# A transpose on one core: one TensorE wait per copying engine and step, a loop meant to fit one instruction fetch of 16 KB, and stores issued right behind their closing copy

## The chip, the cores and the metric

One core of one Trainium2 chip. The metric is device time in microseconds, median of several executions; the kernel before took 1264.57 us (three runs, 1264.06 to 1268.05). Profiles are single executions whose span, from first to last instruction, is about 2 us shorter than the time.

## The reference

```python
def setup_inputs():
    return {"x": np.random.randn(8192, 8192).astype(np.float32)}

def reference(x):
    return np.transpose(x)
```

268.4 MB have to be read and 268.4 MB written.

## The kernel before

The input goes through in 128 steps, each a tile of 128 rows by 4096 columns (2 MiB). TensorE transposes it in 32 blocks of 128 x 128 into four PSUM banks of eight; ScalarE copies banks 0 and 2, VectorE banks 1 and 3, into registers of SBUF ("windows"). Eight windows are open at a time and nine exist; each gathers eight steps, so that a store writes rows of 4 KB, and one closes per step. ScalarE issues all stores and, but for the first three, all loads.

```python
    NIN, NREG = 3, 9
    s_bank = [nc.alloc_semaphore(f"s_bank{q}") for q in range(NR // 2)]     # four banks
    # ...
        def transposes(k):
            nc.tensor.sem_inc(s_ld[k], -16).wait_op(s_ld[k], 16, "sem-ge")
            for h in range(NR // 2):
                nc.tensor.sem_inc(s_bank[h], -1).wait_op(s_bank[h], 1, "sem-ge")
                for b in range(2 * B):
                    # ... one transpose into bank h
                tr.then_inc(s_pe, 1)
    # ...
        with nc.Fori(0, T // NIN + 1, engines=pe, head_slot={pe[0]: 0}) as turn:
            with nc.tensor.If(turn > 0):
                transposes(NIN - 1)
            nc.tensor.wait_ge(s_id, 2)
            for k in range(NIN - 1):
                transposes(k)
    # ...
        for t, (s, c) in enumerate(chunks):
            closing = []
            for h in range(NR // 2):
                e = h % 2
                eng = (nc.scalar, nc.vector)[e]
                # ... open windows; wait for a free register (s_st)
                eng.wait_ge(s_pe, t * NR // 2 + h + 1)
                before = []
                if e == 0:
                    before, closing = closing, []
                # ... the copies of bank h; windows that end here go into `closing`
                for k in before:
                    store(*k)
            for k in closing:
                store(*k)
            if t + NIN < T:
                nc.scalar.wait_ge(s_pe, (t + 1) * NR // 2)
                load(t + NIN)
```

Of the kernel before, what the change touches and what calls it, by code (L numbers as in the profile page):

```python
# [24 lines left out]
def wide_dma(nc, eng, queue, out, in_):  # L25


    return eng.add_instruction(
        mybir.InstDMACopy(
            mode="Copy",  # L30
            name=nc.get_next_instruction_name(),
            engine=eng.engine,
            ins=[physical(in_)],
            outs=[physical(out)],
            queue=queue,
        )
    )


@with_exitstack  # L40
def kernel(
    ctx: ExitStack,
    tc: tile.TileContext,
    x: bass.AP,
    out: bass.AP,
):







    nc = tc.nc
    P = 128
    N, M = x.shape
    assert x.shape == out.shape[::-1]
    dt = x.dtype

    S = 32  # L60
    B = 4
    W = 8
    NR = S // B
    NIN = 3
    NREG = 9
    CH = N // P
    J = S * P

    with tc.tile_critical():  # L69
        nc.alloc_sbuf_tensor("pad", [P, 32], dt)  # L70
        ident = nc.alloc_sbuf_tensor("ident", [P, P], dt).ap()
        ins = [nc.alloc_sbuf_tensor(f"in{k}", [P, J], dt).ap() for k in range(NIN)]
        SIZE = B * W * P
        regs = nc.alloc_sbuf_tensor("regs", [P, NREG * SIZE], dt).ap()
        pss = [nc.alloc_psum_tensor(f"ps{k}", [P, 2 * B * P], dt).ap() for k in range(NR // 2)]

        s_id = nc.alloc_semaphore("s_id")
        s_ld = [nc.alloc_semaphore(f"s_ld{k}") for k in range(NIN)]
        s_st = [nc.alloc_semaphore(f"s_st{k}") for k in range(NREG)]
        s_bank = [nc.alloc_semaphore(f"s_bank{q}") for q in range(NR // 2)]  # L80
        s_pe = nc.alloc_semaphore("s_pe")
        s_cp = [nc.alloc_semaphore("s_cpa"), nc.alloc_semaphore("s_cpv")]

        nc.gpsimd.memset(ident, 0.0).then_inc(s_id, 1)  # L84
        nc.gpsimd.wait_ge(s_id, 1)
        nc.gpsimd.affine_select(  # L86
            out=ident,
            in_=ident,
            compare_op=mybir.AluOpType.not_equal,
            fill=1.0,  # L90
            base=0,
            pattern=[[-1, P]],
            channel_multiplier=1,
        ).then_inc(s_id, 1)

        chunks = [(s, c) for s in range(M // J) for c in range(CH)]

        def load(t):
            s, c = chunks[t]
            (nc.sync if t < NIN else nc.scalar).dma_start(  # L100
                out=ins[t % NIN], in_=x[c * P:(c + 1) * P, s * J:(s + 1) * J]
            ).then_inc(s_ld[t % NIN], 16)





        def transposes(k):
            nc.tensor.sem_inc(s_ld[k], -16).wait_op(s_ld[k], 16, "sem-ge")
            for h in range(NR // 2):  # L110
                nc.tensor.sem_inc(s_bank[h], -1).wait_op(s_bank[h], 1, "sem-ge")  # L111
                for b in range(2 * B):
                    j = (2 * h + b // B) * B * P + b % B
                    tr = nc.tensor.transpose(  # L114
                        pss[h][:, b * P:(b + 1) * P],
                        ins[k][:, j:j + B * P - B + 1:B],
                        ident,
                    )
                tr.then_inc(s_pe, 1)



        T = len(chunks)
        assert T % NIN == NIN - 1
        pe = [nc.tensor.engine]
        for h in range(NR // 2):
            nc.tensor.sem_inc(s_bank[h], 1)
        with nc.Fori(0, T // NIN + 1, engines=pe, head_slot={pe[0]: 0}) as turn:
            with nc.tensor.If(turn > 0):
                transposes(NIN - 1)  # L130
            nc.tensor.wait_ge(s_id, 2)
            for k in range(NIN - 1):
                transposes(k)

        for t in range(NIN):
            load(t)

        copied = [0, 0]
        free = list(range(NREG))
        stored = [0] * NREG  # L140
        window = {}

        def store(q, e, count):
            t0, r, parts = window.pop(q)
            nc.scalar.wait_ge(s_cp[e], count)
            base = 0
            for s, a, z in parts:
                rows = (z - a) * P
                j0 = s * J + q * B * P
                dst = out[j0:j0 + B * P, a * P:a * P + rows]  # L150
                dst = dst.rearrange("(q b) i -> q b i", q=P)
                src = regs[:, r * SIZE + base:r * SIZE + base + B * rows]
                base += B * rows
                if any(stored):
                    st = wide_dma(nc, nc.scalar, "qActDynamicHW", dst, src)
                else:
                    st = nc.scalar.dma_start(
                        out=dst, in_=src.rearrange("q (b i) -> q b i", b=B)
                    )
                st.then_inc(s_st[r], 16)  # L160
                stored[r] += 1
            free.append(r)

        def closes(w, t):
            t0, r, parts = w
            return t + 1 == t0 + sum(z - a for _, a, z in parts)

        for t, (s, c) in enumerate(chunks):
            closing = []
            for h in range(NR // 2):  # L170
                e = h % 2
                eng = (nc.scalar, nc.vector)[e]

                place = []
                for q in (2 * h, 2 * h + 1):
                    if q not in window:



                        span = (q - c) % W + 1  # L180
                        r = free.pop(0)
                        parts = [(s, c, min(c + span, CH))]
                        if c + span > CH and t + span < T:
                            parts.append((s + 1, 0, c + span - CH))
                        window[q] = (t, r, parts)
                        if stored[r]:
                            eng.wait_ge(s_st[r], 16 * stored[r])
                    t0, r, parts = window[q]
                    k = [p[0] for p in parts].index(s)
                    base = r * SIZE + B * P * sum(z - a for _, a, z in parts[:k])  # L190
                    _, a, z = parts[k]
                    place.append((base + (c - a) * P, (z - a) * P))
                ends = [q for q in (2 * h, 2 * h + 1) if closes(window[q], t)]
                gap = place[1][0] - place[0][0]
                runs = [(0, 1)]
                if place[0][1] != place[1][1] or abs(gap) >= 2 ** 15:
                    runs = [(0,), (1,)]
                eng.wait_ge(s_pe, t * NR // 2 + h + 1)  # L198
                before = []
                if e == 0:  # L200
                    before, closing = closing, []
                for u in runs:
                    off, dist = place[u[0]]
                    dims = [list(regs.ap[0]), [gap, len(u)], [dist, B], [1, P]]
                    o = bass.AP(regs.tensor, regs.offset + off, dims)
                    i = pss[h][:, u[0] * B * P:(u[-1] + 1) * B * P]
                    i = i.rearrange("p (l b i) -> p l b i", b=B, i=P)
                    cp = nc.scalar.copy(out=o, in_=i) if e == 0 else nc.vector.tensor_copy(out=o, in_=i)  # L208
                    mine = [q for q in ends if q - 2 * h in u]
                    if mine:  # L210
                        cp.then_inc(s_cp[e], 1)
                        copied[e] += 1
                        closing += [(q, e, copied[e]) for q in mine]
                    if u is runs[-1]:
                        if mine:
                            eng.wait_ge(s_cp[e], copied[e])
                            eng.sem_inc(s_bank[h], 1)
                        else:
                            cp.then_inc(s_bank[h], 1)
                for k in before:  # L220
                    store(*k)
            for k in closing:
                store(*k)
            if t + NIN < T:
                nc.scalar.wait_ge(s_pe, (t + 1) * NR // 2)
                load(t + NIN)
        for r in range(NREG):
            nc.sync.wait_ge(s_st[r], 16 * stored[r])
# [30 lines left out]
```

## Time and profile before

| | kernel before |
|---|---|
| time, median of the first three runs | 1264.57 us |
| span of the profiled run | 1263.0 us |
| TensorE / VectorE / ScalarE busy | 747.5 / 316.0 / 262.9 us |
| bytes read + written, mean rate | 536.9 MB, 425 GB/s |
| from step to step, mid-run | 9.76 us |

Read the page from the engine shares down: when no engine is busy over 60% and the DMA row is all nines, the next question is what the DMA engines lose and where. "DMA share" is the mean over the core's 16 DMA engines. The lines are shown inside the prediction.

### The profile page before, as it was taken

To read this page: it belongs to the slowest core of one execution; us is meant where nothing else is said; L and a number is where in the kernel's file an instruction comes from. 1 tells how busy PE (TensorE), PEld (TensorE's weight loads), DVE (VectorE), ACT (ScalarE), POOL (GpSimd) and SP (SyncE) were. 2 spreads that over 40 slices of the span, in tenths; PEclk is the share of its full clock that TensorE was granted. 3 is DMA by queue.
4 is the path that set the end of the run, shared out by engine and by line. 5 is a ranking of instruction groups with operands and counts; after the bars stand their busy time and mean duration, and the time that the engine had idled before them with its cause. 6 is when DMAs were issued, how large, how long until landed. Compare 5 with 4: busy or idle time off the path is not lost. (4 is left out here: it accounts for less than half of the span.)

```text
span 1263.0 us, 10220 instructions
## 1 busy us (share of the span) xinstructions
PE 747.5 (59%) x4096; PEld 727.0 (58%) x4096; DVE 316.0 (25%) x311; ACT 262.9 (21%) x321; POOL 0.7 (0%) x6
## 2 busy tenths in 40 slices
PE   5665565565556555665556655656556655656561
PEld 5665555565556555665555655656556655656561
DVE  2322222222222222223222222222222222222220
ACT  2312121122212211222212121122212121122120
POOL 0000000000000000000000000000000000000000
PEclk9867877777776867677776686776877777776865
DMA  9999999999999999999999999999999999999998
GB/s 367 430 426 426 426 428 430 429 431 430 429 428 430 430 430 428 430 429 429 430 421 420 428 429 427 427 426 428 427 431 429 431 429 429 429 430 429 430 429 364
DMA packets 39275, 536.98 MB, mean 425 GB/s; under 512 B 4321, under 2 KB 4833, under 8 KB 6241
## 3 DMA queue, kind: packets, MB, share of 16 engines
q10 hardware_dynamic: 38832, 530.60, 98.9%
q1 hardware_dynamic: 432, 6.29, 1.2%
q14 instruction: 10, 0.07, 0.0%
q8 instruction: 1, 0.02, 0.0%
HBM read 268.44 MB, written 268.44 MB: 425 GB/s over the span
## 5 line engine op out<-in xcount | busy, mean ns | idle before, releaser
L114 PE MATMUL ps<-ident,in 128*128 128x128 f32 x4096 | 747.5, 365 | 489.0 <-PEq L111 489.0
L114 PEld LDWEIGHTS ps<-ident,in 128*128 128x128 f32 x4096 | 727.0, 219 | 509.3 <-issue 509.3
L208 DVE COPY regs<-ps 128x1024 f32<-128x1024 f32 (+1 forms) x311 | 316.0, 1034 | 921.8 <-PE ps L114 707.6
L208 ACT COPY regs<-ps 128x1024 f32<-128x1024 f32 (+1 forms) x320 | 261.6, 843 | 972.4 <-PE ps L114 693.6
L208 ACT ACT_TABLE_LOAD x1 | 1.3, 1283 | 0.9 <-SPq L69 0.9
L86 POOL TENSOR_SCALAR_AFFINE_SELECT ident<-ident 128x128 f32<-128x128 f32 x1 | 0.3, 294 | 0.2 <-POOL ident L84 0.2
L84 POOL MEMSET ident<- 128x128 f32 x1 | 0.2, 205 | 0.5 <-SPq L69 0.5
L243 POOL MEMSET const-bfloat16-1.0<- 128x1 bf16 x1 | 0.1, 103 | 0.0
L243 POOL MEMSET const-uint8-127<- 128x1 uint8 x1 | 0.1, 103 | 0.0
L243 POOL MEMSET const-float32-0.0<- 128x1 f32 x1 | 0.1, 99 | 0.2 <-issue 0.2
L243 POOL MEMSET const-float32-1.0<- 128x1 f32 x1 | 0.1, 99 | 0.0
## 6 DMA issues: line engine op xcount, KB each, us to landing
in<-in_x_dram ACTq DMA_DIRECT2D x125, 2048.0 KB, 22.5
out_dram<-regs ACTq DMA_DIRECT2D x114, 2048.0 KB, 18.3
out_dram<-regs ACTq DMA_DIRECT2D x4, 1792.0 KB, 15.3
in<-in_x_dram SPq DMA_DIRECT2D x3, 2048.0 KB, 13.1
out_dram<-regs ACTq DMA_DIRECT2D x4, 1536.0 KB, 14.3
out_dram<-regs ACTq DMA_DIRECT2D x4, 1280.0 KB, 15.0
out_dram<-regs ACTq DMA_DIRECT2D x4, 1024.0 KB, 14.5
out_dram<-regs ACTq DMA_DIRECT2D x4, 768.0 KB, 15.1
```

Of the source, the lines that this page charges most:

```text
L84: nc.gpsimd.memset(ident, 0.0).then_inc(s_id, 1)
L86: nc.gpsimd.affine_select(out=ident, in_=ident, compare_op=mybir.AluOpType.not_equal, fill=1.0, base=0, pattern=[[-1, P]], channel_multipl ...
L114: tr = nc.tensor.transpose(pss[h][:, b * P:(b + 1) * P], ins[k][:, j:j + B * P - B + 1:B], ident,)
L208: cp = nc.scalar.copy(out=o, in_=i) if e == 0 else nc.vector.tensor_copy(out=o, in_=i)
L243: nc = _bacc.Bacc("TRN2", target_bir_lowering=False, num_devices=1)
```

## The change

TensorE is to wait twice per step instead of four times, its program is to fit the first block of instructions fetched (so the placing of the loop's head, `head_slot`, is dropped), and each store is to leave as soon as its data is complete. "Block" stands here and below for what one instruction fetch of TensorE's brings: the traces of both kernels have one fetch on queue q8, of 16 KB.

```diff
-        s_bank = [nc.alloc_semaphore(f"s_bank{q}") for q in range(NR // 2)]
+        s_bank = [nc.alloc_semaphore("s_banka"), nc.alloc_semaphore("s_bankv")]
 ...
             for h in range(NR // 2):
-                nc.tensor.sem_inc(s_bank[h], -1).wait_op(s_bank[h], 1, "sem-ge")
+                if h < 2:
+                    n = NR // 4
+                    nc.tensor.sem_inc(s_bank[h], -n).wait_op(s_bank[h], n, "sem-ge")
 ...
-        for h in range(NR // 2):
-            nc.tensor.sem_inc(s_bank[h], 1)
-        with nc.Fori(0, T // NIN + 1, engines=pe, head_slot={pe[0]: 0}) as turn:
+        for e in range(2):
+            nc.tensor.sem_inc(s_bank[e], NR // 4)
+        nc.tensor.wait_ge(s_id, 2)
+        with nc.Fori(0, T // NIN + 1, engines=pe) as turn:
             with nc.tensor.If(turn > 0):
                 transposes(NIN - 1)
-            nc.tensor.wait_ge(s_id, 2)
 ...
-                before = []
-                if e == 0:
-                    before, closing = closing, []
+                closing = []
 ...   (copies of bank h; s_bank[h] becomes s_bank[e])
-                for k in before:
+                for k in closing:
                     store(*k)
-            for k in closing:
-                store(*k)
```

More of the change, by code (lines that the diff above doesn't have):

```diff
@@ L168 @@
         for t, (s, c) in enumerate(chunks):
-            closing = []
             for h in range(NR // 2):
@@ L216 @@
                             eng.wait_ge(s_cp[e], copied[e])
-                            eng.sem_inc(s_bank[h], 1)
+                            eng.sem_inc(s_bank[e], 1)
                         else:
-                            cp.then_inc(s_bank[h], 1)
-                for k in before:
+                            cp.then_inc(s_bank[e], 1)
+                for k in closing:
                     store(*k)
-            for k in closing:
-                store(*k)
             if t + NIN < T:
```

## The prediction

> **What bounds the kernel now.** I read the page first: engine shares, then the forty slices, then the bytes of the DMA queues. It says at once that no compute engine is the bound and that the DMA engines are.
>
> ```profile
> span 1263.0 us, 10220 instructions
> PE 747.5 (59%) x4096; PEld 727.0 (58%) x4096; DVE 316.0 (25%) x311; ACT 262.9 (21%) x321; POOL 0.7 (0%) x6
> DMA  9999999999999999999999999999999999999998
> GB/s 367 430 426 426 426 428 430 429 431 430 429 428 430 430 430 428 430 429 429 430 421 420 428 429 427 427 426 428 427 431 429 431 429 429 429 430 429 430 429 364
> q14 instruction: 10, 0.07, 0.0%
> HBM read 268.44 MB, written 268.44 MB: 425 GB/s over the span
> ```
>
> The DMA row is 9 in every slice but the last, and the rate stands at 420 to 431 GB/s in 38 slices of 40. The kernel must move 268.44 MB in and 268.44 MB out; 536.9 MB at 430 GB/s are 1248.5 us. The span is 1263.0, so about 14.5 us are all that is not full-rate transfer. The slices say where they lie (a slice is 31.6 us): the first, at 367, loses (430-367)/430 of 31.6 = 4.6 us; the last, at 364, loses 4.8; the 38 between lose about 5 together, some 3.5 of it in small sags of 1 to 4 GB/s and 1.4 in the two slices at 421 and 420, where the input's column half changes and the stores are short.
>
> Next I read the list of waits, to see whether anything waits for TensorE that matters, and then the time line of four steps.
>
> ```profile
> DVE regs L208 <- PE ps L114: 707.6, 204, 13.6
> ACT regs L208 <- PE ps L114: 693.6, 176, 9.7
> PE ps L114 <- PEq L111: 489.0, 127, 9.9
> ACT regs L208 <- DMA out_dram<-regs: 276.8, 50, 9.4
> DVE regs L208 <- DMA out_dram<-regs: 212.7, 30, 7.9
> ```
>
> TensorE waits 489.0 us in 127 waits, once before each of the 128 steps but one, 3.85 us each. The wait is booked to its own sequencer, at the line that waits for the load; the time line shows the rhythm:
>
> ```profile
> 602.25 6.43 PE L114 MATMUL ps<-ident,in 128*128 128x128 f32 x32 [3.55 <-PEq L111]
> 612.01 6.64 PE L114 MATMUL ps<-ident,in 128*128 128x128 f32 x32 [3.34 <-PEq L111]
> 621.77 5.37 PE L114 MATMUL ps<-ident,in 128*128 128x128 f32 x32 [3.12 <-PEq L111]
> ```
>
> Steps start 9.76 us apart whether TensorE took 6.64 or 5.37 us. A step moves 2 MiB in and 2 MiB out, 4.194 MB; over 9.76 us that is 430 GB/s. The step is the time of its transfers. Inside a step the 32 transposes come in one unbroken row: the three bank waits after the first cost nothing that the view can separate.
>
> Last, the end of the run in narrow windows (columns: window, its length, busy us of PE, PEld, DVE, ACT, POOL, granted clock, DMA share, GB/s):
>
> ```profile
> 1232.00:1234.00 2.00, 2.00 (x11) 2.00 (x10) 0.54 (x1) 0.83 (x2) 0.00 (x0) 0.50 1.02 434
> 1234.00:1236.00 2.00, 2.00 (x12) 2.00 (x11) 0.75 (x2) 0.83 (x2) 0.00 (x0) 0.55 0.85 360
> 1236.00:1238.00 2.00, 0.42 (x4) 0.23 (x2) 1.29 (x2) 0.24 (x1) 0.00 (x0) 1.00 0.45 187
> 1238.00:1240.00 2.00, 0.00 (x0) 0.00 (x0) 0.00 (x0) 0.00 (x0) 0.00 (x0) 0.81 1.10 454
> 1260.00:1261.00 1.00, 0.00 (x0) 0.00 (x0) 0.00 (x0) 0.00 (x0) 0.00 (x0) 0.50 0.16 66
> 1261.00:1263.00 2.00, 0.00 (x0) 0.00 (x0) 0.00 (x0) 0.00 (x0) 0.00 (x0) 0.50 0.00 0
> ```
>
> Here is the one place after the start where the DMA engines run dry: 1234 to 1238, at shares of 0.85 and 0.45.
>
> [...]So the first aim of the change, a program within one block, would matter if TensorE's loop refetched each turn. This trace speaks against that: 10 packets on the instruction queue in the whole span, for all engines, against 42 jumps back of the loop (43 turns of three steps).
>
> **The change part by part.**
>
> TensorE's waits. A step has four waits for PSUM banks now, and two after: one before the first bank for both of ScalarE's copies of the step before, one before the second for both of VectorE's. Per loop turn that removes 3 x 2 = 6 semaphore instructions or waits of about 3 x (1 + 4 + 64) = 207 (a transpose is a weight load and a matmul), leaving 201. Time gained: none on the path, since whatever TensorE saves becomes a longer wait for the load. What the coarser wait could cost: the first transposes of a step now need ScalarE's second copy of the step before. In the time line, TensorE ends at 608.68; ScalarE's last copy of the step ends at 608.72 and VectorE's at 610.07; the next step starts at 612.01. ScalarE is done 3.3 us before it is needed. In the worst pattern shown there (a copy held by a store until 626.45) the last ScalarE copy ends at 628.71 for a start at 631.53, 2.8 us of room. Cost 0.
>
> The fetch block and the wait for the identity moved ahead of the loop. The identity is ready at 1.7 us, the first load only just before TensorE's first instruction at 9.9 us. Gain 0 at the start, 0 later by the packet count above.
>
> The stores. Before, a store closed by the first bank is issued behind ScalarE's second copy of the step, two banks later; one closed by the second bank likewise behind that copy. After, each is issued right behind its closing copy. In the middle of the run this brings 2 of 8 stores forward by about two banks, some 3.4 us, and 2 by less. The order on the queue stays the same (store, then the step's load), and the queue is never empty there, so an earlier issue only lengthens the stay in the queue. Gain 0. In the last step it is different: all eight open windows close together, and nothing is loaded any more. ScalarE's copies of the first bank end at about 1232.8, but the first of the eight stores is issued only at 1236.36, and the DMA engines dry out meanwhile. With the change two stores, of 7 and 6 chunks by 256 KB = 1.79 + 1.54 (in units of 1024 KB: 3.3 in all, 3.41 MB, 7.9 us of work at 430 GB/s), are issued from about 1232.9 on, while the queue still has work. The dry time goes: (1-0.85) x 2 + (1-0.45) x 2 = 0.3 + 1.1 = 1.4 us; from the rates, (430-360)/430 x 2 + (430-187)/430 x 2 = 0.3 + 1.1 = 1.4 again.
>
> Sum: 0 + 0 + 0 - 1.4 = -1.4 us, from 1264.6 to 1263.2.
>
> **The rivals.**
>
> One: ScalarE now stands still in front of a store closed by VectorE's first bank until that copy is done, before its own second copy. VectorE is itself held by a store up to 7.9 us (30 waits). Then ScalarE's second copy, and with it TensorE's next start and the next load, come later. Against it: the load was always issued behind that store, so it moves by one copy, 0.6 to 1.1 us, in at most 2 steps of 8; and loads take 22.5 us from issue to landing, more than two steps, so they wait in a queue that others fill. If it bit each time, 32 steps by 1 us would be +32 us, 1295 us, slower by 2.5%.
>
> Two: the loop did refetch, or the four waits did stall TensorE, and TensorE gets faster. Its 489 us of idle time take it all: 0 us. For a real gain DMA itself would have to be freed, and that the bytes forbid: even with no loss at all it would be 1248.5 plus about 5 us of first and last latency, under 1% below now.
>
> Three: earlier stores mix with loads differently and the sags between 420 and 428 GB/s get better or worse. They are 5 us in all, so this moves the time by 2 or 3 us either way and I cannot tell which.
>
> **Range and chances.** The centre is 1264.6 - 1.4 = 1263.2, which I put at 1263.1, as an earlier fill may mend a sag. The three runs before spread from 1264.06 to 1268.05; with rival three's 2 to 3 us I take 1260 to 1266.5. Faster by 2% would be 1239.3, below the floor of the bytes at 430 GB/s: 0.01. Slower by 2% needs rival one nearly in full: 0.02. Within 2%: 0.97.
>
> **What would show it right or wrong.** The GB/s row should stay near 430 in the middle, steps 9.76 us apart. Near the end no window with a DMA share of 0.45; the first of the last stores issued some 3.5 us sooner than TensorE's last transpose; the span 1 to 2 us shorter. TensorE's idle time should stay near 490 us, with the same few instruction packets. The prediction is wrong if the middle slices fall below 420 (rival one: longer waits of TensorE for copies, dry DMA windows in mid-run), or if the span falls by more than 5 us, for then some wait that I call hidden did set the pace.

That 430 GB/s is the most to be had is the estimate from the slices, of which none is above 431 in that trace. The "about 5 us of first and last latency" fit the narrow windows of the same trace: against 430 GB/s the first 4 us lose 2.6 (0, 66, 197 and 360 GB/s), and 1260 to 1263 loses 2.8 (66, then 0 twice).

## The result, and the profile after

The changed kernel takes 1264.29 us (median of six, 1263.53 to 1265.31), the kernel before 1264.66 us (six, 1264.06 to 1268.05). The ratio of the fast runs is 0.9994, 95% interval 0.9981 to 1.0007: the same. (Such a ratio is the mean time of one kernel's fast runs over that of the other's in the same rounds, so not quite the ratio of the medians.) The predicted 1263.1 us, 1260 to 1266.5, held the time. Whether the gain of 1.4 us that it was built on came, the times alone cannot tell: the interval runs from 2.4 us faster to 0.9 slower. The traces tell, below: it did not.

From the page of the changed kernel:

```profile
span 1262.9 us, 9961 instructions
PE 742.7 (59%) x4096; PEld 721.8 (57%) x4096; DVE 316.1 (25%) x311; ACT 263.0 (21%) x321; POOL 0.7 (0%) x6
GB/s 381 429 430 420 429 431 428 430 429 431 428 430 430 431 428 429 430 430 430 426 425 414 429 430 429 430 430 430 428 430 430 431 428 430 430 430 429 430 427 339
q14 instruction: 9, 0.07, 0.0%
```

The span is 0.1 us shorter. The middle is at 430 GB/s as before. One slice, where the input's column half changes, reads 414 (before: 420), which is below the 420 that the prediction named as a sign of rival one; but the 38 middle slices together lose 3.7 us against 430 GB/s here and 4.6 before, so this is no sign of a slower middle. The last slice is at 339, where it was 364: the end carries less, not more. From its list of waits (who waited for whom, us in total, times, longest):

```profile
PE ps L117 <- PEq L114: 493.1, 128, 8.5
ACT regs L208 <- DMA out_dram<-regs: 260.3, 45, 9.2
DVE regs L208 <- DMA out_dram<-regs: 214.8, 30, 7.9
ACT regs L208 <- DVE regs L208: 47.1, 13, 4.0
```

TensorE's idle time is 493 us where it was 489. ScalarE now waits 47.1 us for VectorE's copies, a row that the kernel before does not have; its waits for stores went down by 16.5. Rival one of the prediction is thus in the trace, and costs nothing that the times resolve.

The end of the changed kernel in the narrow windows that the prediction used, and then the one window of the kernel before that the prediction left out:

```profile
1232.00:1234.00 2.00, 2.00 (x11) 2.00 (x11) 1.12 (x2) 0.25 (x1) 0.00 (x0) 0.50 0.90 383
1234.00:1236.00 2.00, 1.87 (x11) 1.67 (x9) 0.19 (x2) 0.00 (x0) 0.00 (x0) 0.68 1.09 453
1236.00:1238.00 2.00, 0.00 (x0) 0.00 (x0) 1.27 (x2) 1.07 (x2) 0.00 (x0) 1.00 0.89 373
1238.00:1240.00 2.00, 0.00 (x0) 0.00 (x0) 0.00 (x0) 0.00 (x0) 0.00 (x0) 0.67 1.09 463
1250.00:1260.00 10.00, 0.00 (x0) 0.00 (x0) 0.00 (x0) 0.00 (x0) 0.00 (x0) 0.50 0.71 292
```

```profile
1250.00:1260.00 10.00, 0.00 (x0) 0.00 (x0) 0.00 (x0) 0.00 (x0) 0.00 (x0) 0.50 1.01 417
```

The hole at 1234 to 1238 is filled, as predicted. A larger one has opened right at the end: from 1250 to 1260 the share falls from 1.01 to 0.71. The time lines show that the cause was as predicted: the first of the last stores was issued four microseconds sooner, 3.4 us sooner when counted from the start of TensorE's last step. The changed kernel, then the kernel before (start, length, queue, line, what):

```profile
1229.19 6.68 PE L117 MATMUL ps<-ident,in 128*128 128x128 f32 x32 [3.29 <-PEq L114]
...
1232.36 4.00 ACTq L28 DMA_DIRECT2D out_dram<-regs  x4
```

```profile
1229.77 6.65 PE L114 MATMUL ps<-ident,in 128*128 128x128 f32 x32 [3.31 <-PEq L111]
...
1236.36 15.47 ACTq L28 DMA_DIRECT2D out_dram<-regs  x8
```

So the DMA engines were given work sooner and finished no sooner. A share of 0.71 in the last ten microseconds says that some engines were done early and others were not, and a mean cannot show which. The landing records can. The trace records sixteen landings for each transfer (4,320 for 270 transfers). And between 20 and 1225 us the packet records of both kernels have sixteen packets of data under way at about nine instants in ten (else mostly 17), a packet of 16 KB taking 0.61 us. So I speak of 16 rings, each of which carries and lands a share of a transfer; the records give no ring a name. The waiting engine goes on at the sixteenth landing: TensorE's first transpose of a step starts 0.3 us behind it in 127 of 128 steps of the kernel before and in 126 of the changed one. I read the landing times of every transfer out of both traces (not a view of the profile; "spread" is the sixteenth minus the first, all in us):

```
                        last load,   its      last store,   its      from the one
                        16th landing spread   16th landing  spread   to the other
kernel before           1229.48      3.37     1261.72       1.27     32.24
changed kernel          1228.89      5.51     1261.61       4.60     32.72
```

In both kernels the rings run several microseconds apart. In the kernel before, the rings that were ahead ran dry around 1236 us and waited (8 packets under way at 1236 us, 4 at 1237, 16 at 1238); the one behind did not, as I read it, and the spread shrank to 1.27 us. In the changed kernel the rings ahead went on (16 packets under way at 1236 and 1237 us), and were done 4.6 us before the last one (3 packets under way at 1258 us, 1 at 1260). The last ring took no less time.

At the start there is a second thing that the prediction had not seen. TensorE's first transposes, before and after:

```profile
9.92 9.61 PE L114 MATMUL ps<-ident,in 128*128 128x128 f32 x64 [9.92 <-PEq L111]
```

```profile
8.46 6.14 PE L117 MATMUL ps<-ident,in 128*128 128x128 f32 x32 [8.46 <-PEq L114]
```

By the packet records, one instruction fetch of 16 KB ran at 5.95 us in the kernel before and at 20.10 us in the changed one; it takes 0.93 us. In the kernel before the first load's sixteenth landing came 1.41 us behind the fifteenth, in the changed kernel 0.01 us. While this fetch runs, 15 packets of data are under way in either trace, where else 16 are. So the fetch block did matter for the start, by 1.46 us, and still the span shrank by only 0.1. (The page shows this fetch in its line "q8 instruction: 1, 0.02", which the prediction did not read.)

### The profile page after: what moved, and what is told of

The parts are those of the page before. It is cut to its first block, busy times and chain, and to the rows that moved or that the text cites. A ratio compares the mean times of both kernels' runs of the same rounds, so it can differ in the third digit from the quotient of the medians.

```text
span 1262.9 us, 9961 instructions
## 1 busy us (share of the span) xinstructions
PE 742.7 (59%) x4096; PEld 721.8 (57%) x4096; DVE 316.1 (25%) x311; ACT 263.0 (21%) x321; POOL 0.7 (0%) x6
## 2 busy tenths in 40 slices
DMA packets 39274, 536.98 MB, mean 425 GB/s; under 512 B 4320, under 2 KB 4832, under 8 KB 6240
## 5 line engine op out<-in xcount | busy, mean ns | idle before, releaser
L117 PE MATMUL ps<-ident,in 128*128 128x128 f32 x4096 | 742.7, 364 | 493.1 <-PEq L114 493.1
```

What stands on the lines that cost most here:

```text
L117: tr = nc.tensor.transpose(pss[h][:, b * P:(b + 1) * P], ins[k][:, j:j + B * P - B + 1:B], ident,)
```

## The experiments

The theories. **A**: each transfer is finished by its last ring, and the last ring sets every wait and the end; dry time on other rings is worth nothing. **B**: the mean DMA share sets the time; the 1.4 us were gained and lost again elsewhere. Later **D** joined: the last ring is last because it alone carries the instruction fetches. (It turned out to hold for ScalarE's fetches only; see the end of this part.) Twelve kernels ran, all correct. Ratios are against the kernel before, in the same rounds on the same chip.

| run | time, median | ratio of fast runs | 95% interval |
|---|---|---|---|
| stores alone | 1264.39 | 0.9994 | 0.9981 to 1.0006 |
| TensorE's part alone | 1264.52 | 0.9994 | 0.9982 to 1.0007 |
| uneven rings | 1382.47 | 1.053 | 1.0497 to 1.0562 |
| even control | 1275.15 | 1.0078 | 1.0066 to 1.0091 |
| three rings more | 1340.16 | 1.0331 | 1.0295 to 1.0367 |
| sixteen rings more | 1321.20 | 1.0162 | 1.0145 to 1.0179 |
| TensorE a quarter more | 1264.48 | 1.0015 | 0.9982 to 1.0048 |
| loop twice as long | 1264.78 | 0.9998 | 0.9986 to 1.0011 |
| ScalarE 1,500 more instructions | 1271.19 | 1.0045 | 1.0029 to 1.006 |
| three probes, one run each | 1267.39, 1267.94, 1273.48 | | |

### The two parts alone

The stores alone, on the kernel before:

```diff
-                before = []
-                if e == 0:
-                    before, closing = closing, []
+                closing = []
 ...
-                for k in before:
+                for k in closing:
                     store(*k)
-            for k in closing:
-                store(*k)
```

> The kernel before with the new place of the stores alone; TensorE's four waits a step and its loop stay as they were. Theory A (my theory after reading both traces: each transfer is cut over 16 rings, the sixteenth ring to land it sets every wait and the end, and that ring was never dry at the end of the kernel before): no gain, 1264.0 to 1265.0 us; the last load to the last landing takes 32.2 us as before or up to 0.5 more, although the windows around 1236 us no longer show a DMA share of 0.45, and the sixteen landings of the last store stay spread over more than 3 us where the kernel before has 1.3. Theory B (the prediction's own step: the dry 1.4 us are worth 1.4 us and something else in the changed kernel took 1 us of it back): 1263.2 us, last load to last landing 30.8 us.

TensorE's part alone is the rest of the change, with the stores placed as before.

> The kernel before with TensorE's part alone: two waits a step, the loop in one fetch block, the wait for the identity ahead of the loop; stores placed as before. Theory A: 1264.0 to 1265.0 us, the same as before; TensorE's first transpose at 8.4 us instead of 9.9 (the 16 KB instruction fetch moves from 6 us to 20 us and no longer delays one ring of the first load), which buys nothing because the DMA rings have work all the while; the spread of the last store's sixteen landings near 1.3 us and a dry window near 1236 us as in the kernel before. Theory C (the 1.4 us sooner start is worth 1.4 us): 1263.2 us.

Neither part moves the time by more than the interval, which is 1.6 us wide to either side and so does not rule out 1.4 us by itself. The end of the run with TensorE's part alone:

```profile
1232.00:1234.00 2.00, 2.00 (x11) 2.00 (x11) 1.12 (x2) 0.24 (x1) 0.00 (x0) 0.50 0.52 221
1234.00:1236.00 2.00, 1.57 (x11) 1.38 (x9) 0.49 (x2) 1.07 (x2) 0.00 (x0) 0.85 0.27 115
1236.00:1238.00 2.00, 0.00 (x0) 0.00 (x0) 0.97 (x2) 0.00 (x0) 0.00 (x0) 1.00 0.63 261
```

The hole is 0.96 + 1.46 + 0.74 = 3.2 us deep here, more than twice that of the kernel before. The landing records of this run, and of all others whose large transfers are unchanged, settle theory B:

```
                              stores  last load,   its      last store,   its      from the one
                                      16th landing spread   16th landing  spread   to the other
kernel before                 late    1229.48      3.37     1261.72       1.27     32.24
TensorE's part alone          late    1228.89      6.37     1261.13       1.27     32.24
probe on the kernel before    late    1229.09      4.77     1261.86       2.56     32.77
changed kernel                early   1228.89      5.51     1261.61       4.60     32.72
stores alone                  early   1229.83      7.14     1262.55       4.61     32.72
probe on the changed kernel   early   1228.56      5.84     1261.30       4.65     32.74
TensorE a quarter more        early   1228.45      5.74     1261.16       4.62     32.71
loop twice as long            early   1227.12      2.90     1259.33       2.88     32.21
1,500 more instructions       early   1233.65      9.06     1265.88       4.62     32.23
1,500 more, with the probe    early   1234.96      9.72     1267.22       4.64     32.26
```

The end takes 32.2 or 32.7 us with early stores as with late ones, and 32.24 us with a hole of 1.4 us as with one of 3.2. The hole lies on rings that are not last. What makes the difference between 32.2 and 32.7 is not the place of the stores. It fits the half microsecond that an instruction fetch of ScalarE costs the ring that carries it (below). All but the last two of these runs have such a fetch near 1236 or 1237 us. As I read it, it costs time only where its ring is the last one by then, and the fetch before it, near 1014 us, tells: in the five runs at 32.7 that fetch made the last landing late by 0.18 to 0.50 us (in the probe on the changed kernel it only drew level with the last ring), in the three others by less than 0.02. The last two runs have no fetch there, and end at 32.23 and 32.26. This is read from the traces of ten runs; no run was built to test it.

Of the run with TensorE's part alone, theory A had said that the spread at the end would be near 1.3 (1.27) and that TensorE would start at 8.4 us (8.47, with the fetch at 19.65). With the stores alone it started at 9.66, with the fetch at 5.69. The sooner start belongs to TensorE's part. That it buys nothing is harder to show: by the thirteenth load the kernel before stands at 103.19 us, the changed one at 102.28, TensorE's part alone at 102.64, the stores alone at 102.45, and the kernel with the long loop, which starts late (TensorE at 9.56), at 101.75. A late start alone does not decide where a run stands by then. Both parts lie within 1 us of each other, and the timing resolves 1.6.

### Loading some rings more than others

Theory A says that work put on a few rings costs as much as the same packet put on all. The packet records have as many packets of 4 bytes as landings (4,320 in the kernel before), so the packet counts on the pages give the landings of the transfers that these runs add: 24 added stores of three partitions add 144 packets, that is 3 of data and 3 of 4 bytes each, and 24 of sixteen partitions add 768, 16 and 16 each. A store cut into 112 + 8 + 8 partitions has 16 more landings than a whole one (384 packets in 24), which fits 16 + 8 + 8; one cut into 64 + 32 + 32 has 32 more (768), three times 16. I take the landings of a transfer for its rings. Which rings a transfer with fewer than sixteen takes, and how its partitions are shared out, the counts do not show. That the two parts of 8 partitions go to the same eight rings, which then carry one packet more than without the cut, was the assumption; theory A's 14.6 us for the uneven run rest on it. A packet of 16 KB takes 0.61 us in the packet records of both kernels.

First try, the kernel before with 24 of its 2 MiB stores cut by partitions:

```diff
+                if rows == W * P and len(parts) == 1 and cut[0] < 24 and stored[r] >= 2:
+                    cut[0] += 1
+                    for lo, hi in ((0, 112), (112, 120), (120, 128)):    # control: (0, 64), (64, 96), (96, 128)
+                        wide_dma(nc, nc.scalar, "qActDynamicHW", dst[lo:hi], src[lo:hi]).then_inc(s_st[r], 16)
+                        stored[r] += 1
+                    continue
```

> The kernel before with 24 of its 2 MiB stores cut in three by partitions, 112 + 8 + 8, same bytes. [...]One partition is a packet of 16 KB, 0.61 us on its ring. Theory A (the last ring sets the time): 24 x 0.61 = 14.6 us more on the loaded rings, less the up to 3.4 us by which they may have been ahead: 1275.8 to 1279.2 us. Theory B (the mean DMA share sets the time): no change beyond the cost of two more issues per store, 1264 to 1266 us.

> Control for the uneven run: the same 24 stores cut in three as 64 + 32 + 32 partitions[...]. Both theories: 1264 to 1266 us; what it costs over the kernel before is the price of two more DMA issues for 24 stores.

The rates of the uneven run, then of its even control:

```profile
GB/s 384 429 428 428 430 393 364 353 373 362 347 361 344 351 369 387 430 430 419 429 425 426 417 429 419 426 428 412 429 426 421 428 428 432 420 429 428 430 406 346
```

```profile
GB/s 363 429 428 428 428 388 400 408 413 423 428 427 422 423 430 429 430 429 429 430 426 413 430 430 430 428 430 429 429 431 430 429 429 429 429 432 430 429 424 351
```

Both missed. The uneven cut of the same bytes costs 62 us in its fastest run (1326.98) and 129 in its slowest (1394.42; four of the six are called slow, which on one core means only over 1.5% above the fastest run of the same kernel), where theory A had 11 to 15 and theory B none. The even control costs 10 us, where both theories had about none. The cuts change more than the balance: there are 48 transfers more. The direction speaks for A, if the assumption holds; the sizes belong to neither, and what a cut transfer costs here stays open. So the next pair leaves the stores whole and adds a small one:

```diff
+                if rows == W * P and len(parts) == 1 and extra[0] < 24 and stored[r] >= 3:
+                    nc.scalar.dma_start(out=scr[extra[0]], in_=src[0:12:4, 0:B * W * P]).then_inc(s_st[r], 16)
+                    # sixteen rings: src[0:128:8, 0:B * W * P]
+                    stored[r] += 1
+                    extra[0] += 1
```

> The kernel before, and behind 24 of its 2 MiB stores one more small store of 3 partitions by 16 KB into a scratch tensor in HBM. Three partitions go over 3 rings, so three of the sixteen rings get one packet of 16 KB more, 0.61 us each time; 1.18 MB in all. Theory A (the last ring sets the time): 24 x 0.61 = 14.6 us less the lead that these rings may have, up to 3.4 us: 11 to 15 us more than the kernel before, 1276 to 1280 us. Theory B (the mean DMA share sets it): 1.18 MB at 430 GB/s are 2.7 us: 1267.5 us.

> The same with 16 partitions by 16 KB: every one of the sixteen rings gets the packet, 6.29 MB in all. Both theories: 6.29 MB at 430 GB/s are 14.6 us, 1279 us. What tells the theories apart is the ratio of ring3 to ring16: theory A 0.75 to 1, theory B 3/16.

Fast runs: 1300.8 and 1312.9 us with three rings loaded, 1284.9 and 1286.1 with sixteen. By the ratios, 3.3% against 1.6%: three sixteenths of the bytes cost twice as much. Theory B, which had the three-ring run at a fifth of the other, is out. (Each ratio rests on two of six runs: the six spread over 52 us with three rings and over 69 with sixteen, and the other four of each are called slow. But even the fastest three-ring run is 36 us over the kernel before, where theory B had 2.7.) Theory A had it at three quarters to the same, and is too mild. The rates of the three-ring run (profiled in a slow run, at 1347.3 us) and of the sixteen-ring run (a fast one):

```profile
GB/s 375 428 430 429 428 428 430 429 426 400 383 367 394 395 385 395 370 409 420 392 401 410 408 384 391 395 383 400 394 371 423 422 413 426 391 406 374 399 336 339
```

```profile
GB/s 373 428 429 427 425 428 424 426 426 427 430 429 429 428 425 418 429 420 431 430 422 416 430 427 431 429 431 424 433 426 431 428 430 428 429 425 431 427 421 339
```

The three-ring run stays near 395 GB/s for most of the rest of the run, long after the last of the 24 additions, which was issued at 414 us. Its landing records have three rings, as many as were loaded, 7.5 to 15.6 us behind the first from 318 us on, and twelve within 1.9; the 24 packets come to 14.6 us. So the lag is of the size that theory A has, and the loss of time is larger. What costs time while rings are that far apart I have not separated, and a slow run must not be read for more than that.

### TensorE's work and its loop

The changed kernel with a quarter more for TensorE, and with a loop of six steps instead of three:

```diff
-                for b in range(2 * B):
+                for b in list(range(2 * B)) * (1 + (h == 3)):
```

```diff
-        with nc.Fori(0, T // NIN + 1, engines=pe) as turn:
+        with nc.Fori(0, T // (2 * NIN) + 1, engines=pe) as turn:
             with nc.tensor.If(turn > 0):
                 transposes(NIN - 1)
+                for k in range(NIN):
+                    transposes(k)
```

> The changed kernel with the eight transposes of the last bank done twice in every step, 40 instead of 32, a quarter more work for TensorE. If TensorE's 493 us of idle time are all wait for loads, as the prediction says, this costs nothing: 1264 to 1265.5 us, TensorE's busy time up by about 185 us and its idle time down by as much. If TensorE's pace or its waits set any part of the step, up to 128 x 1.4 = 180 us more.

> The changed kernel with TensorE's loop twice as long: six steps a turn, 6 x 67 = 402 instructions[...]. If a jump back beyond one block refetches each turn, there are 21 or more instruction packets of 16 KB instead of 1, and a longer gap of TensorE once per turn; each packet holds one ring for 0.93 us, so by theory A up to 21 x 0.93 = 20 us more if they fall on the last ring, and nothing if they fall on one that is ahead. If nothing is refetched: the same packets as before, 1264 to 1265 us.

```profile
PE 793.4 (63%) x5120; PEld 772.7 (61%) x5120; DVE 316.5 (25%) x311; ACT 263.0 (21%) x321; POOL 0.7 (0%) x6
PE ps L117 <- PEq L114: 440.4, 128, 8.5
```

1024 more transposes cost nothing: 1264.48 us in the median, five of six runs at 1263.8 to 1264.6 and one at 1279.97 that I cannot explain. (TensorE's busy time rose by 51 us and its idle time fell by 53, and not by 185: its granted clock was 0.848 here and 0.749 in the changed kernel.) A wait or two less per step was never going to show. The instruction queues of the run with the long loop:

```profile
q14 instruction: 9, 0.07, 0.0%
q8 instruction: 1, 0.02, 0.0%
```

A loop of 402 instructions refetches nothing in 21 jumps back: one fetch of 16 KB in the run, at 5.60 us as in the kernel before. So the block matters for that one fetch, early or at 20 us, and not for the turns. (At 8 KB per 125 to 132 instructions, an estimate from ScalarE's fetches, 402 instructions are about 26 KB, more than the 16 KB fetched.) A loop of more than 402 instructions was not tried.

### Which ring is last, and why

Behind the last store of either kernel, sixteen tiny loads on semaphores of their own:

```diff
+        for k in range(1, 17):
+            nc.scalar.dma_start(out=pad[0:k, k:k + 1], in_=x[0:k, k:k + 1],
+                                allow_slow_non_contiguous=True).then_inc(s_pr[k], 16)
```

> The changed kernel with sixteen tiny loads behind its last store, of 1, 2, ... 16 partitions by 4 bytes, each on its own semaphore. [...]No theory of the cause needs a certain ring; if the lag is a property of a ring, the same ring is last here and in the kernel before; if it comes from chance delays that no ring ever makes good, the last ring differs. The spread of the sixteen landings at the end should be 3 us or more, as in the changed kernel. Time 1266 to 1272 us.

> The same sixteen tiny loads behind the last store of the kernel before. The spread at the end should be near 1.3 us, since its rings draw level while the queue is dry. Time 1266 to 1272 us.

The probe adds 272 packets, all under 512 bytes, to the page of the run with 1,500 more instructions for ScalarE: two for each of the 136 partitions of the sixteen loads, one of data and one of a landing. So a load of k partitions lands k times. That each load takes the rings of the one before and one more was the assumption, not shown by the counts. The landings of the first loads (us; each record's first number, which I do not count as a landing, is left out):

```
                              1 partition    2 partitions
probe on the changed kernel   1256.84        1257.02  1261.48
probe on the kernel before    1259.51        1259.69  1262.04
```

If the assumption holds, the ring that joins with the second partition is the last of all in both, 4.46 us behind the first ring in the changed kernel and 2.35 in the kernel before. A landing as late is in each of the fifteen loads of two partitions and more, which fits the assumption. In the changed kernel the one that joins with the fourth partition is late too (1261.01). That one ring is last twice is hardly chance. What does it carry that others do not? The packet records have nine instruction fetches of 8 KB in the body of either run, 0.31 us each (in the traces of the two kernels 15 packets of data are under way during such a fetch, 16 at single instants, where else 16 are; during the last of the kernel before, at 1236.6 us, 3), and the last landing of the loads falls behind its steady 9.76 us in single steps just after some of them (changed kernel: fetches at 762.1 and 1014.5, steps of 0.40 and 0.50 us too much at 769.7 and 1023.9). That is theory D, and it has a test: more instructions for ScalarE, all waits that are already fulfilled. The 12 fetches expected of 1,500 instructions are an estimate: in the trace of the changed kernel ScalarE's come one per 125 to 132 of its instructions.

```diff
-                nc.scalar.wait_ge(s_pe, (t + 1) * NR // 2)
+                for _ in range(25):
+                    nc.scalar.wait_ge(s_pe, (t + 1) * NR // 2)
```

> The changed kernel with 1,500 more instructions on ScalarE's sequencer, waits that are already fulfilled, twelve in each step ahead of the load; [...]about 12 more fetches of 8 KB beside the 9 of the changed kernel. Theory D: the instruction fetches all ride on one ring, the one that the probes found last in both kernels (the second), and each holds it for its 0.31 us or a little more, which is never made good. Then 12 x 0.31 to 12 x 0.5 = 3.7 to 6 us more, 1268 to 1270.3 us, each fetch visible as a step of the last landing that is 0.3 to 0.5 us over the steady 9.76 us, and the last landing further behind the fifteenth. Theory E (a fetch of 8 KB is 8 KB among 537 MB, shared by all): no change, 1264 to 1265.5 us, since ScalarE's sequencer has room for twelve waits.

> The same with the sixteen tiny loads behind the last store. Theory D: the second ring is last again, and by more than in the changed kernel's probe, where it was 4.6 us behind the first ring. Theory E: no ring is marked out. Time 1266 to 1273 us.

(The 24 more waits a step of this edit come out as twelve instructions a step: the trace has 2,217 instructions of ScalarE where the changed kernel has 717.)

```profile
q14 instruction: 20, 0.16, 0.0%
```

Eleven more fetches (20 against 9). The time rises by the ratio 1.0045, 5.7 us, which is 0.52 us for each (the interval of the ratio allows 0.33 to 0.69); one of six runs, at 1306.95, is a slow one. In the trace most fetches from 458 us on are followed, 2 to 10 us later, by one step of the last landing that is too long, by 0.48 to 0.53 us mostly (eleven of thirteen; three of the steps are 0.69 to 0.78). Before that the ring is not yet the last by any margin (at 376 us the sixteenth landing is 0.05 us behind the fifteenth) and the fetches leave little or no mark. Seven of them:

```
fetch at            458.1  526.8  743.6  812.4  880.6  1106.6  1176.1
surplus step ends   465.6  534.4  752.4  821.2  890.0  1116.1  1184.9
over 9.76 us by      0.50   0.53   0.50   0.49   0.50    0.50    0.50
```

By the end of the loads the fifteenth ring is 3.88 us behind the first and the sixteenth 9.06: one ring alone fell back. The probe names it, on the same assumption: 1262.95 us for the first ring, 1267.40 for the second, and no other ring is late. One detail of the expectation missed: the second ring is 4.45 us behind the first at the end, no more than in the changed kernel's probe (4.46). The others ran dry before the end here; at the last load the whole spread was 9.72 us against 5.84. Theory E, which had no change, is out.

Theory D holds for ScalarE's fetches and not for all. Counting each engine's instructions between the fetches sorts them: 17 of the 20 come one per 127 instructions of ScalarE on average, the other three (152.2, 545.0 and 897.6 us) one per 127 to 129 of VectorE. The eleven added ones are ScalarE's. VectorE's leave no mark on the last landing here; instead a ring further ahead falls back, by about 0.75 us after the fetch at 545.0 (from 0.98 to about 1.7 us behind the first). So VectorE's instructions seem to ride on another ring. And a fetch costs time only while its ring is the last: in the changed kernel two of ScalarE's five up to the last load were followed by such a step, in the kernel before none of the four from 330 us on; with TensorE's part alone it was one of VectorE's (893.9) that was, by 0.99 us.

At the last load the sixteenth landing was 2.9 to 9.7 us behind the first in the ten runs of the table above. No run here shows such a lag of the last ring made good there: after the first sixteen loads no step of the last landing was more than 0.22 us under 9.76.

Larger steps come where the input's column half changes (1.3 us in one step at 691 us in the changed kernel); their cause was not looked for. Why a fetch that takes 0.31 us costs 0.5 is open.

## Why the prediction was right and wrong

- **The bound.** Right: the step is the time of its transfers; a quarter more work for TensorE cost nothing.
- **TensorE's waits, 0.** Right: its idle time is 493.1 us where 489.0 was, and the coarser wait delays nothing.
- **The fetch block, 0 at the start.** Wrong in mechanism: the block's fetch moved from 5.95 to 20.10 us and TensorE started 1.46 us sooner. Right in what came of it, as far as the times resolve. That the loop refetches nothing was right.
- **The stores in mid-run, 0.** Right as far as the times resolve, and the new wait of rival one is there with 47.1 us and is hidden.
- **The stores at the end, -1.4 us.** This is the step that failed. The hole closed as described, and the stores left when described. But "the dry time goes: ... 1.4 us" took a mean over 16 rings for the time of each. The last ring was not dry; from the last load to the last store it took 32.24 us before and 32.72 after. (A slip on the way cost nothing: 1.79 and 1.54 are not units of 1024 KB, which would be 1.75 and 1.5; the 3.41 MB that follow are right.)
- **The sum.** In the two profiled runs, at the thirteenth load the changed kernel is 0.91 us ahead, at the last load 0.59 ahead, at the end of the stores 0.11. All three are smaller than what two runs of one kernel differ by. The range held by luck: because the terms were small, not because the one gain in it was real.

No version beats both kernels clear of noise. Fewer instructions on ScalarE, which the runs seem to point to, were not built, and would bring little: the two steps in the changed kernel come to 0.9 us, with the fetch at 1237 us to about 1.4, an estimate from that one trace and an upper one, since the next ring is not far behind.

## What to carry to other kernels

When the DMA engines are the bound, ask for the last ring, not for the mean share: look at the spread of one transfer's landings before counting a dry window as time to be had. Here the 1.4 us of dry time were worth nothing: from the last load to the last store it took 32.24 us with them and 32.72 without. On such a kernel an engine off the critical path can still cost through the length of its program: here eleven more fetches of ScalarE's instructions cost 5.7 us, 0.52 us each. Taking waits away from an engine that idled 40% of the time only made its remaining wait longer here (493 us where it was 489).
